# A two-layer transformer trunk in fp32 on one core: seven products of half blocks for eight in the last layer's second MLP product, and rotary tables loaded per layer

## The chip, the cores and the metric

The kernel runs on one core of one Trainium2 chip. The metric is the device time of one execution in microseconds. The kernel before takes 1665.89 us, the median of three runs (1664.36 to 1666.99).

## The reference

A latent stream x of 512 tokens and a context of 256 tokens, each 1024 wide, go through two layers. A layer normalises and modulates its input, projects it to three groups of attention heads (windowed, neighbourhood and latent), projects the heads' outputs back, and adds them with a gate. Then comes a squared-ReLU MLP of width 4096:

```python
def sq_relu_mlp(h, w1, w2):
    return jnp.square(jax.nn.relu(h @ w1)) @ w2
...
    x = x + mod_x[5] * sq_relu_mlp(modulate(rmsnorm(x, norm2_g[l]), mod_x[3], mod_x[4]),
                                   w_mlp_in[l], w_mlp_out[l])
    if not last:
        ctx = ctx + mod_c[5] * sq_relu_mlp(...)
return rmsnorm(x, final_norm_g)
```

In the last layer the context is not updated any more, so its MLP works on 512 tokens, in the first layer on 768. All data are float32.

## The kernel before

Each product of the large matrices is made of three matmuls, since TensorE gets operands in the shorter format fp32r: an operand is split into a high part (a cast on ACT) and a low part (the difference, on DVE), and high x high, high x low and low x high are added up in PSUM. `load_split` (L449) does that for a weight tile of 1024 columns: DMA to `raw`, ACT's cast to `wh` (L457), DVE's subtraction to `wl` (L458). The tiles `wh` and `wl` share a pool of five buffers, `w4`.

The MLP goes over 32 chunks of 128 hidden features in eight groups of four (L1054). `mlp1` makes a chunk: 24 matmuls in the last layer (8 pieces of the input, three each, L1083 to L1085) into a `psd` bank, then ReLU on ACT (L1090), the square on ACT as high part `uh` (L1091), the square on POOL (L1092) and the low part `ul` on DVE (L1093). `mlp2` makes a group's share of the second product: for each half of the 1024 output columns, four banks (`pss`, `pss`, `psv`, `psa`), one for each 128 tokens, get 4 chunks x 3 matmuls of 512 columns each (L1117 to L1119), that is 96 in a group. `resid` (L716) then multiplies a bank by the gate on DVE (L719) and adds it to x on POOL (L720). The loop at the end issues `mlp1(g + 1)` ahead of `mlp2(g)`. The last group goes through a path of its own (L1124), token tile by token tile, with split weights `wfh`, `wfl`.

A scheduler that is part of the build orders the instructions of each engine, from the order of the program, the buffers of the pools (`CAPS`) and its own estimate of durations; on the chip each engine works through its list in that order and waits at semaphores. So a change of a pool's size moves instructions in the whole program. `FENCE` delays a few DMAs at the start by a DVE copy of one column. The rotary table and the mask of the windowed heads are loaded once, in layer 0, to the pool of constants (`const`, L145, and L850).

```python
        mlp1(0)
        for g in range(NG):
            if g + 1 < NG:
                mlp1(g + 1)
            if g == 0:
                gates = load_gate(l, 5, 1 if last else 2)
            mlp2(g)
```

## Time and profile before

| | |
|---|---|
| median of three runs | 1665.89 us |
| profiled execution | 1664.7 us, of it a span of 1662.8 us |
| PE (matmul) busy | 1615.0 us, 97%, 8994 instructions |
| DVE busy | 1010.4 us, 61% |
| ACT busy | 684.2 us, 41% |
| POOL busy | 610.5 us, 37% |
| mean granted TensorE clock | 0.994 |
| chain that ended last | PE 89%, DVE 6%, DMA 2%, ACT 1% |

The span is the time from the first to the last instruction; the execution's time lies 1.9 us above it. Busy shares are averages over stages that have different limits. PE, DVE, ACT and POOL are TensorE's matmuls, VectorE, ScalarE and GpSimd. L12 is line 12 of the kernel. The chain of work that ended last is followed back from the last instruction, at each step to what released it.

### The profile page before, as it was taken

What the parts mean: (1) busy time and instruction counts of PE and PEld (TensorE: products, weight loads), DVE (VectorE), ACT (ScalarE), POOL (GpSimd) and SP (SyncE); (2) the same over time, 40 slices, a digit from 0 to 9 for tenths busy, and PEclk for the clock granted to TensorE, in tenths of its full rate; (3) what the DMA queues carried; (4) which work ended last, traced back from release to release, by engine and by line L of the source; (5) the groups of instructions that cost most, each with busy time, mean ns of one, the idle gap of its engine ahead of it and who ended that gap; (6) DMA issues with size and microseconds to landing.
All of it is one profiled execution on the core that took longest, in us unless ns stands there. A gap on an engine that the chain in (4) does not pass through costs nothing.

```text
span 1662.8 us, 24078 instructions
## 1 busy us (share of the span) xinstructions
PE 1615.0 (97%) x8994; PEld 1354.3 (81%) x8994; DVE 1010.4 (61%) x1995; ACT 684.2 (41%) x1342; POOL 610.5 (37%) x564
## 2 busy tenths in 40 slices
PE   6999999999899999999999999999999899999997
PEld 3888788776798988988989789878776788888886
DVE  3665865687787576444544866786686643344445
ACT  4544466656631312212223155536755522233332
POOL 1111643553433353341533441153453333333335
PEclk9999999999999999999999999999999999999999
DMA  9553411220154333334333712221120233333331
GB/s 319 179 167 112 134 35 26 67 65 13 33 184 134 120 115 114 115 102 125 90 106 116 236 51 74 62 60 39 42 82 15 66 98 91 102 101 97 93 106 72
DMA packets 156422, 164.47 MB, mean 99 GB/s; under 512 B 8960, under 2 KB 111368, under 8 KB 156304
## 3 DMA queue, kind: packets, MB, share of 16 engines
q1 hardware_dynamic: 156304, 162.92, 32.1%
q8 instruction: 71, 1.16, 0.3%
q14 instruction: 47, 0.39, 0.1%
HBM read 155.53 MB, written 2.12 MB: 95 GB/s over the span
## 4 chain that ended last, share of the span: by engine, by line
PE 89%; DVE 6%; DMA 2%; ACT 1%; issue 1%; POOL 0%; SPq 0%; POOLq 0%; DVEq 0%; ACTq 0%
PE psd L1083 9%; PE psd L1084 9%; PE psd L1085 9%; PE psv L669 5%; PE pss L611 5%; PE pst L660 5%; PE pss L1117 3%; PE pss L1118 3%; PE pss L1119 3%; PE psd L474 3%; PE psd L475 3%; PE psd L476 3%; PE pst L1119 2%; PE pst L1118 2%; PE psv L1118 2%; PE psv L1119 2%
## 5 line engine op out<-in xcount | busy, mean ns | idle before, releaser
L720 POOL TENSOR_TENSOR xlat<-xlat,rtmp 128x512 f32<-128x512 f32 x159 | 234.3, 1497 | 267.7 <-DVE rtmp L719 264.5
L458 DVE TENSOR_TENSOR wl<-raw,wh 128x1024 fp32r<-128x1024 f32 (+1 forms) x168 | 219.1, 1305 | 184.0 <-issue 72.2
L457 ACT CAST wh<-raw 128x1024 fp32r<-128x1024 f32 (+1 forms) x168 | 174.8, 1041 | 301.1 <-PE pst L1119 175.4
L1083 PE MATMUL psd<-hT,wh 128*128 128x384 f32 (+2 forms) x752 | 264.8, 353 | 3.9 <-DVE hT L421 3.9
L1084 PE MATMUL psd<-hT,wl 128*128 128x384 f32 (+2 forms) x752 | 264.2, 351 | 2.5 <-DVE wl L458 2.5
L1085 PE MATMUL psd<-hT,wh 128*128 128x384 f32 (+2 forms) x752 | 265.2, 353 | 0.1
L635 POOL TENSOR_TENSOR prob<-prob,sm 128x512 f32<-128x512 f32 (+3 forms) x110 | 126.9, 1161 | 256.3 <-DVE sm L628 175.8
L1092 POOL TENSOR_TENSOR relu<-relu 128x384 f32<-128x384 f32 (+1 forms) x96 | 97.6, 1018 | 314.1 <-ACT uh L1091 299.6
L1090 ACT ACTIVATE relu<-psd 128x384 f32<-128x384 f32 (+1 forms) x93 | 49.1, 528 | 279.4 <-PE psd L1085 276.4
L627 ACT ACTIVATE prob<-prob,m 128x513 f32<-128x513 f32 (+6 forms) x160 | 121.2, 758 | 94.3 <-DVE m L622 69.2
L1083 PEld LDWEIGHTS psd<-hT,wh 128*128 128x128 f32 x752 | 141.4, 188 | 15.7 <-DVE hT L421 4.4
L1093 DVE TENSOR_TENSOR ul<-relu,uh 128x384 fp32r<-128x384 f32 (+1 forms) x96 | 59.2, 617 | 152.7 <-POOL relu L1092 152.7
L1084 PEld LDWEIGHTS psd<-hT,wl 128*128 128x128 f32 x752 | 141.4, 188 | 12.8 <-DVE wl L458 3.2
L1085 PEld LDWEIGHTS psd<-hT,wh 128*128 128x128 f32 x752 | 141.3, 188 | 9.7 <-DVE hT L423 0.3
L282 DVE SCALAR_TENSOR_TENSOR acc<-araw,consts,acc 128x512 f32<-128x512 f32 x140 | 116.9, 860 | 15.0 <-DMA araw<-in_w_ada_dram 14.0
L660 PEld LDWEIGHTS pst<-consts,prob 128*128 128x128 f32 x688 | 77.8, 141 | 48.3 <-issue 37.5
L660 PE MATMUL pst<-consts,prob 128*128 128x128 f32 x688 | 114.2, 282 | 2.4 <-POOL prob L635 1.3
L476 PE MATMUL psd<-hT,wl 128*128 128x384 f32 (+1 forms) x280 | 97.1, 347 | 1.1 <-DVE wl L458 1.1
L474 PE MATMUL psd<-hT,wh 128*128 128x384 f32 (+1 forms) x280 | 97.8, 349 | 0.2 <-DVE rtmp L719 0.2
L475 PE MATMUL psd<-hT,wh 128*128 128x384 f32 (+1 forms) x280 | 97.1, 347 | 0.0
L664 ACT COPY pT<-pst 128x512 f32<-128x512 f32 x124 | 70.9, 585 | 62.8 <-PE pst L660 62.6
L1118 PE MATMUL pss<-wl,uh 128*128 128x512 f32 x224 | 87.4, 390 | 0.0
(265 smaller groups left out, 3576.9 us busy)
## 6 DMA issues: line engine op xcount, KB each, us to landing
raw<-in_w_mlp_in_dram SPq DMA_DIRECT2D x64, 512.0 KB, 4.0
raw<-in_w_mlp_out_dram SPq DMA_DIRECT2D x64, 512.0 KB, 3.8
araw<-in_w_ada_dram SPq DMA_DIRECT2D x112, 256.0 KB, 4.7
raw<-in_w_in_dram SPq DMA_DIRECT2D x24, 512.0 KB, 5.3
raw<-in_w_ada_dram SPq DMA_DIRECT2D x24, 512.0 KB, 3.9
raw<-in_w_ada_dram SPq DMA_DIRECT2D x32, 256.0 KB, 5.7
raw<-in_w_out_dram SPq DMA_DIRECT2D x8, 512.0 KB, 3.7
raw<-in_w_out_dram SPq DMA_DIRECT2D x16, 256.0 KB, 3.7
```

The costliest lines, as they stand in the source:

```text
L457: A.copy(hi, raw)
L458: V.tensor_tensor(lo, raw, bc(hi), ALU.subtract)
L474: T.matmul(ps[:, :n], wh[:, k, :], hh[k][:, s0:s0 + n], start=(k == 0), stop=False)
L475: T.matmul(ps[:, :n], wh[:, k, :], hl[k][:, s0:s0 + n], start=False, stop=False)
L476: T.matmul(ps[:, :n], wl[:, k, :], hh[k][:, s0:s0 + n], start=False, stop=(k == KC - 1))
L635: G.tensor_tensor(p_[:, :w_], p_[:, :w_], sm.to_broadcast([P, w_]), ALU.mult)
L660: T.transpose(pt[:, r * P:(r + 1) * P], pts[r][:, pos[r][kb]:pos[r][kb] + P], ident)
L720: (V if fast and (RLAST if fast == "end" and t == 3 else RFAST)[dh] == "V" else G).tensor_tensor(xt[t][:, cs], xt[t][:, cs], tmp, ALU.add)
L1083: T.matmul(o_, wh[:, k, :], hh[k][:, sl], start=(k == 0), stop=False)
L1084: T.matmul(o_, wl[:, k, :], hh[k][:, sl], start=False, stop=False)
L1085: T.matmul(o_, wh[:, k, :], hl[k][:, sl], start=False, stop=(k == KC - 1))
L1118: T.matmul(a_, uh[:, ts_], wl[:, c % 2, :], start=False, stop=False)
```

## The change

In seven of the eight groups of the last layer, two chunks of features and two token halves form a 2 x 2 block of the left matrix (token halves of 256, a11 and a12 the first half of the tokens, chunk by chunk), and two chunks and two column halves of the weights a 2 x 2 block of the right one (b11 and b12 the first chunk, column half by column half). Their product is made by the scheme of Strassen in Winograd's form: seven products of half blocks, four sums on the left and four on the right. `left_seven` and `right_seven` are generators that give one split operand at a time; the left sums and three of the right ones are made on POOL, one of the right ones on DVE. `product` adds the two pairs of chunks of a group in PSUM: 2 pairs x 2 banks x 3 matmuls = 12, seven times a group. Products go by turns to two banks `pss` and to the banks `psv` and `psa`; three of them are copied out by ACT to `pc` tiles (L1226), and the sums that Winograd's form needs at the end are made by further accumulation in the bank and by DVE (L1231). Gate and addition to x follow as before, by new lines (L1236 on DVE, L1237 on POOL) or by `resid`.

`uh` is now the full square of the chunk, made on POOL alone; there is no `ul` in these groups. The weights are loaded to `raw2` tiles. Splits of 256 columns go to `left` tiles (six), of 512 columns to `right` tiles (six). `w4` has four buffers for five, the split input of the MLP is two tiles in place of sixteen, attention outputs have a pool of their own, and rotary table and mask are loaded in each layer to `rA`, behind a copy of one column. The diff, cut:

```diff
-CAPS = {"tm": 4, "rt": 4, "pr": 8, "r0": 16, "re": 9, "raw": 4, "w4": 5, "pT": 4, "xn": 12,
-        "h1": 16, "h2": 16, "pg": 18, "cr": 1, "ct": 8, "kr": 5, "vc": 2, "kc": 8,
-        "up": 4, "u": 16, "wf": 16, "of": 8, "fg": 2, "ga": 4}
+CAPS = {"tm": 4, "rt": 4, "pr": 8, "r0": 16, "re": 9, "raw": 4, "w4": 4, "pT": 4, "xn": 12,
+        "h1": 16, "h2": 2, "pg": 18, "cr": 1, "ct": 8, "kr": 5, "vc": 2, "kc": 8,
+        "up": 4, "u": 16, "ls": 6, "rs": 6, "rw": 6, "pc": 7, "ts": 2, "wf": 16, "of": 8, "fg": 2, "ga": 4, "ot": 8, "rA": 1}
...
-FENCE = {"pw0": 4, "pw1": 6, "w3": 24, "w4": 30, "rA": 31, "mA": 31}
+FENCE = {"pw0": 4, "pw1": 6, "w3": 24, "w4": 4, "rA": 31, "mA": 31}
...
         xns = [norm_xn(g) for g in (groups if (l, which) != (0, 1) else groups[:1])]
         cols = mod_cols(l, which)
         ntok = P * sum(len(g) for g in groups)
-        hh = [page(ntok, F32R, f"hT{which}") for _ in range(KC)] if (l, which) != (0, 1) else []
-        hl = [page(ntok, F32R, f"hT{which}") for _ in range(KC)] if (l, which) != (0, 1) else []
+        hh, hl = [], []
+        if which == 2:
+            hh, hl = [[t_[:, k * ntok:(k + 1) * ntok] for k in range(KC)]
+                      for t_ in (page(KC * ntok, F32R, "hT2"), page(KC * ntok, F32R, "hT2"))]
+        elif l:
+            hh = [page(ntok, F32R, "hT1") for _ in range(KC)]
+            hl = [page(ntok, F32R, "hT1") for _ in range(KC)]
...
         def new_ot(c):
-            OT[c] = (page(nq, F32R, "oth"), page(nq, F32R, "otl"))
+            OT[c] = page2(nq, "ot")
...
         att_B(0)
-        if l == 0:
-            rA = const([2, 512], ropeA, "ropeA")
-            maskA = const([3, P], maskA_in, "maskA")
+        tabA = page(1408, name="ropeA")
+        rA, maskA = view(tabA[:, :1024], [2, 512]), view(tabA[:, 1024:], [3, P])
+        for t_, src, key in ((rA, ropeA, "rA"), (maskA, maskA_in, "mA")):
+            if l == 0:
+                fence(t_[:, 0], key)
+            else:
+                V.tensor_copy(t_[:, 0, 0:1], bc(KB[0][0][:, 0:1]))
+            nc.sync.dma_start(t_, src)
         proj_B(1)
         att_B(1)
         proj_AK()
...
         F0 = [sum(GSZ[:i]) for i in range(len(GSZ))]
         us = {}
 
+        def seven(g):
+            return last and g < len(GSZ) - 1
         def mlp1_chunks(g, c_list):
             work = []
             for i, c in enumerate(c_list):
                 f0 = (F0[g] + c) * P
                 w = load_split(
                     [(ALLP, w_mlp_in[l, :, f0:f0 + P].rearrange("(k p) f -> p k f", p=P))], [KC, P])
-                uh = page(ntok, F32R, "uh")
-                ul = page(ntok, F32R, "ul")
+                if seven(g):
+                    uh, ul = page(ntok, F32, "uh"), None
+                else:
+                    uh, ul = page(ntok, F32R, "uh"), page(ntok, F32R, "ul")
                 us[g, c] = (uh, ul)
                 pss = [(ps_d() if i == 0 else ps_s(), s0, n) for s0, n in halves]
                 work.append((w, pss, uh, ul))
...
                     sl = slice(s0, s0 + n)
                     r_ = prob(n, name="relu")
                     A.activation(r_, ps[:, :n], AF.Relu)
+                    if ul is None:
+                        G.tensor_tensor(uh[:, sl], r_, r_, ALU.mult)
+                        continue
                     A.activation(uh[:, sl], r_, AF.Square)
                     G.tensor_tensor(r_, r_, r_, ALU.mult)
                     V.tensor_tensor(ul[:, sl], r_, bc(uh[:, sl]), ALU.subtract)
...
             T.matmul(a_, uh[:, ts_], wl[:, c % 2, :], start=False, stop=False)
             T.matmul(a_, ul[:, ts_], wh[:, c % 2, :], start=False, stop=fin)
 
+        def left_seven(g, q):
+            n = ntok // 2
+            u0, u1 = us[g, 2 * q][0], us[g, 2 * q + 1][0]
+            a11, a21, a12, a22 = u0[:, :n], u0[:, n:], u1[:, :n], u1[:, n:]
+            def split(src):
+                o_ = page(2 * n, F32R, "left")
+                A.copy(o_[:, :n], src)
+                V.tensor_tensor(o_[:, n:], src, bc(o_[:, :n]), ALU.subtract)
+                return o_
+            e_ = page(n, name="tsum")
+            G.tensor_tensor(e_, a21, a22, ALU.add)
+            yield split(a11)
+            G.tensor_tensor(a21, a11, a21, ALU.subtract)
+            G.tensor_tensor(a11, e_, a11, ALU.subtract)
+            yield split(a12)
+            yield split(a11)
+            yield split(e_)
+            G.tensor_tensor(a12, a12, a11, ALU.subtract)
+            yield split(a21)
+            yield split(a12)
+            yield split(a22)
+        def right_seven(g, q):
+            f0 = (F0[g] + 2 * q) * P
+            r_ = []
+            for dh in range(2):
+                r_.append(view(sbuf(1024, F32, "raw2"), [2, 512]))
+                if g < 2:
+                    V.tensor_copy(r_[dh][:, 0, 0:1], bc(hh[0][:, 0:1]))
+                nc.sync.dma_start(r_[dh], w_mlp_out[l, f0:f0 + 2 * P, dh * 512:(dh + 1) * 512]
+                                  .rearrange("(j p) n -> p j n", p=P))
+            b11, b21, b12, b22 = r_[0][:, 0], r_[0][:, 1], r_[1][:, 0], r_[1][:, 1]
+            def split(src):
+                o_ = page(1024, F32R, "right")
+                A.copy(o_[:, :512], src)
+                V.tensor_tensor(o_[:, 512:], src, bc(o_[:, :512]), ALU.subtract)
+                return o_
+            e_ = page(512, name="tsum")
+            yield split(b11)
+            G.tensor_tensor(b11, b12, b11, ALU.subtract)
+            V.tensor_tensor(e_, b22, b11, ALU.subtract)
+            yield split(b21)
+            yield split(e_)
+            G.tensor_tensor(b21, b21, e_, ALU.subtract)
+            yield split(b11)
+            G.tensor_tensor(b12, b22, b12, ALU.subtract)
+            yield split(b12)
+            yield split(b22)
+            yield split(b21)
+        def mlp2_seven(g):
+            nt = ntok // 256
+            n = ntok // 2
+            nq_ = GSZ[g] // 2
+            ops = [(left_seven(g, q), right_seven(g, q)) for q in range(nq_)]
+            def product(banks, first):
+                for q, (le, ri) in enumerate(ops):
+                    a_, b_ = next(le), next(ri)
+                    for t, ps in enumerate(banks):
+                        ah, al = a_[:, t * P:(t + 1) * P], a_[:, n + t * P:n + (t + 1) * P]
+                        more = dict(skip_group_check=True)
+                        T.matmul(ps, ah, b_[:, :512], start=(first and q == 0), stop=False, **more)
+                        T.matmul(ps, ah, b_[:, 512:], start=False, stop=False, **more)
+                        T.matmul(ps, al, b_[:, :512], start=False, stop=(q == nq_ - 1), **more)
+            def out(banks):
+                res = []
+                for ps in banks:
+                    res.append(page(512, name="pc"))
+                    A.copy(res[-1], ps)
+                return res
+            def add(kept, banks, r, dh):
+                for t, (k_, ps) in enumerate(zip(kept, banks)):
+                    V.tensor_tensor(k_, k_, ps, ALU.add)
+                    resid_in(k_, r * nt + t, dh)
+            def resid_in(k_, t, dh):
+                cs = slice(dh * 512, (dh + 1) * 512)
+                V.tensor_tensor(k_, k_, gates[0 if t < 4 else 1, dh], ALU.mult)
+                G.tensor_tensor(xt[t][:, cs], xt[t][:, cs], k_, ALU.add)
+            fx = [ps_s, ps_s, ps_s][:nt]
+            fy = [ps_v, ps_a] if nt == 2 else [ps_t, ps_t, ps_v]
+            x_ = [f() for f in fx]
+            product(x_, True)
+            p1 = out(x_)
+            y_ = [f() for f in fy]
+            product(y_, True)
+            add(p1, y_, 0, 0)
+            product(x_, False)
+            u2 = out(x_)
+            step(STEPS)
+            y_ = [f() for f in fy]
+            product(y_, True)
+            p5 = out(y_)
+            product(x_, False)
+            add(p5, x_, 1, 1)
+            product(y_, False)
+            add(u2, y_, 0, 1)
+            product(x_, False)
+            for t, ps in enumerate(x_):
+                resid(ps, nt + t, 0, gates)
+            step(STEPS)
         def mlp2(g):
+            if seven(g):
+                return mlp2_seven(g)
```

The order of POOL's instructions in the middle of the last layer's MLP, one group before: squares of four chunks (L1092), and eight additions to x (L720).

```order
L1092 TENSOR_TENSOR relu_14765<-relu_14765 128x512
L1092 TENSOR_TENSOR relu_14803<-relu_14803 128x512
L720 TENSOR_TENSOR xlat_69<-xlat_69,rtmp_14872 128x512
L720 TENSOR_TENSOR xlat_69<-xlat_69,rtmp_14875 128x512
L720 TENSOR_TENSOR xlat_69<-xlat_69,rtmp_14878 128x512
L720 TENSOR_TENSOR xlat_69<-xlat_69,rtmp_14881 128x512
L720 TENSOR_TENSOR xlat_69<-xlat_69,rtmp_14948 128x512
L720 TENSOR_TENSOR xlat_69<-xlat_69,rtmp_14951 128x512
L720 TENSOR_TENSOR xlat_69<-xlat_69,rtmp_14954 128x512
L720 TENSOR_TENSOR xlat_69<-xlat_69,rtmp_14957 128x512
L1092 TENSOR_TENSOR relu_14993<-relu_14993 128x512
L1092 TENSOR_TENSOR relu_15031<-relu_15031 128x512
```

And with the change, twelve rows of a group (uh: left operands, raw2: right operands, pc: products that were kept; L1116 is a chunk's square):

```order
L1162 TENSOR_TENSOR tsum_14315<-uh_13848,uh_13883 128x256
L1164 TENSOR_TENSOR uh_13848<-uh_13848 128x256
L1237 TENSOR_TENSOR xlat_69<-xlat_69,pc_13956 128x512
L1237 TENSOR_TENSOR xlat_69<-xlat_69,pc_13958 128x512
L1237 TENSOR_TENSOR xlat_69<-xlat_69,pc_14056 128x512
L1165 TENSOR_TENSOR uh_13778<-tsum_14296,uh_13778 128x256
L1193 TENSOR_TENSOR raw2_14301<-raw2_14303,raw2_14301 128x512
L1165 TENSOR_TENSOR uh_13848<-tsum_14315,uh_13848 128x256
L1237 TENSOR_TENSOR xlat_69<-xlat_69,pc_14058 128x512
L1199 TENSOR_TENSOR raw2_14303<-raw2_14303 128x512
L1193 TENSOR_TENSOR raw2_14320<-raw2_14322,raw2_14320 128x512
L1169 TENSOR_TENSOR uh_13813<-uh_13813,uh_13778 128x256
```

Between the additions to x stand the sums of the next group's operands now; of these twelve rows eight are new work.

The order of DVE's instructions in the same stretch before: weight splits (L458), low parts of the chunks (L1093) and gate products (L719).

```order
L1093 TENSOR_TENSOR ul_14359<-relu_14385,uh_14358 128x512
L458 TENSOR_TENSOR wl_14469<-raw_14466,wh_14468 128x1024
L1093 TENSOR_TENSOR ul_14397<-relu_14423,uh_14396 128x512
L458 TENSOR_TENSOR wl_14511<-raw_14508,wh_14510 128x1024
L1093 TENSOR_TENSOR ul_14435<-relu_14461,uh_14434 128x512
L458 TENSOR_TENSOR wl_14541<-raw_14538,wh_14540 128x1024
L1093 TENSOR_TENSOR ul_14473<-relu_14499,uh_14472 128x512
L458 TENSOR_TENSOR wl_14587<-raw_14584,wh_14586 128x1024
L719 TENSOR_TENSOR rtmp_14568<-pss_14504,gates_91 128x512
L719 TENSOR_TENSOR rtmp_14571<-pss_14505,gates_91 128x512
L719 TENSOR_TENSOR rtmp_14574<-psv_14506,gates_91 128x512
L458 TENSOR_TENSOR wl_14617<-raw_14614,wh_14616 128x1024
```

And with the change (L1159 splits a left operand, L1189 a right one, L1231 adds a PSUM bank to a kept product, L1236 multiplies by the gate):

```order
L1231 TENSOR_TENSOR pc_14056<-pc_14056,pss_13912 128x512
L1189 TENSOR_TENSOR right_14139<-raw2_13940,right_14139 128x512
L1236 TENSOR_TENSOR pc_14056<-pc_14056,gates_91 128x512
L1159 TENSOR_TENSOR left_14298<-uh_13778,left_14298 128x256
L1231 TENSOR_TENSOR pc_14058<-pc_14058,pss_13913 128x512
L1189 TENSOR_TENSOR right_14306<-raw2_14301,right_14306 128x512
L1159 TENSOR_TENSOR left_14317<-uh_13848,left_14317 128x256
L1236 TENSOR_TENSOR pc_14058<-pc_14058,gates_91 128x512
L1189 TENSOR_TENSOR right_14325<-raw2_14320,right_14325 128x512
L1231 TENSOR_TENSOR pc_14024<-pc_14024,psv_14028 128x512
L1159 TENSOR_TENSOR left_14342<-uh_13813,left_14342 128x256
L1231 TENSOR_TENSOR pc_14026<-pc_14026,psa_14029 128x512
```

The splits of the next group's first operands stand between the additions that close this group. By count, the whole program has 84 matmuls fewer (8400 to 8316), 204 instructions more on DVE (1786 to 1990), 182 more on ACT and 98 more on POOL.

## Rows read from the trace of the kernel before

**Rows 1.** The page: span, busy time and share of each engine xinstructions, clock by slice.

```profile
span 1662.8 us, 24078 instructions
...
PE 1615.0 (97%) x8994; PEld 1354.3 (81%) x8994; DVE 1010.4 (61%) x1995; ACT 684.2 (41%) x1342; POOL 610.5 (37%) x564
...
PEclk9999999999999999999999999999999999999999
```

**Rows 2.** Chain that ended last, second layer's MLP: start us, us, what.

```profile
1361.54 0.45 PE pss L1117 x2
1405.06 0.45 PE pss L1117 x2
...
1622.66 0.45 PE pss L1117 x2
```

**Rows 3.** Windows, same stage: length, busy (count) of PE, PEld, DVE, ACT, POOL, PEclk, DMA.

```profile
1340.00:1400.00 60.00, 60.00 (x267) 49.67 (x266) 23.45 (x26) 18.18 (x24) 19.43 (x15) 1.00 0.32 97
...
1580.00:1640.00 60.00, 60.00 (x267) 49.67 (x266) 28.65 (x35) 16.73 (x26) 25.17 (x20) 1.00 0.27 88
```

**Rows 4.** Groups of ACT by line and shape: xcount, busy us, mean ns, idle before.

```profile
L457 ACT CAST wh<-raw 128x1024 fp32r<-128x1024 f32 x160 | 167.8, 1049 | 301.1 <-PE pst L1119 175.4 <-PE psa L1119 100.5 <-DMA raw<-in_w_in_dram 7.2
L664 ACT COPY pT<-pst 128x512 f32<-128x512 f32 x124 | 70.9, 585 | 62.8 <-PE pst L660 62.6
...
L1090 ACT ACTIVATE relu<-psd 128x512 f32<-128x512 f32 x31 | 18.6, 600 | 101.8 <-PE psd L1085 101.8
...
L1134 ACT CAST wfh<-raw 128x512 fp32r<-128x512 f32 x16 | 9.4, 621 | 16.8 <-DMA raw<-in_w_mlp_out_dram 16.8
```

**Rows 5.** Timeline of POOL, second layer's MLP: start us, us, line, operation, tiles.

```profile
1303.20 0.74 POOL L423 TENSOR_TENSOR hT<-tf,hT 128x256 fp32r<-128x256 f32 x1 [0.96 <-DVE hT L421]
...
1319.10 2.04 POOL L1092 TENSOR_TENSOR relu<-relu 128x512 f32<-128x512 f32 x2 [4.94 <-ACT uh L1091]
1324.28 1.04 POOL L1092 TENSOR_TENSOR relu<-relu 128x512 f32<-128x512 f32 x1 [3.14 <-ACT uh L1091]
...
1358.95 6.07 POOL L720 TENSOR_TENSOR xlat<-xlat,rtmp 128x512 f32<-128x512 f32 x4 [6.43 <-DVE rtmp L719]
...
1625.97 2.20 POOL L720 TENSOR_TENSOR xlat<-xlat,rtmp 128x512 f32<-128x512 f32 x1 [1.92 <-DVE rtmp L719]
1629.40 1.29 POOL L720 TENSOR_TENSOR xlat<-xlat,rtmp 128x512 f32<-128x512 f32 x1 [1.23 <-DVE rtmp L719]
```

**Rows 6.** Timeline of DVE, same stage, same columns.

```profile
1309.37 0.43 DVE L423 TENSOR_TENSOR hT<-tf,hT 128x256 fp32r<-128x256 f32 x1
...
1359.54 0.69 DVE L719 TENSOR_TENSOR rtmp<-psv,gates 128x512 f32<-128x512 f32 x1
...
1624.60 0.69 DVE L1135 TENSOR_TENSOR wfl<-raw,wfh 128x512 fp32r<-128x512 f32 x1 [2.57 <-ACT wfh L1134]
...
1625.81 1.22 DVE L458 TENSOR_TENSOR wl<-raw,wh 128x1024 fp32r<-128x1024 f32 x1
1626.94 1.78 DVE L1135 TENSOR_TENSOR wfl<-raw,wfh 128x512 fp32r<-128x512 f32 x1
```

**Rows 7.** Timeline of PE: the last matmul of the program.

```profile
1653.55 0.39 PE L1147 MATMUL psa<-wfh,ul 128*128 128x512 f32 x1
```

**Rows 8.** Waits of PE: releaser, us in total, times, longest; the first two.

```profile
PE psa L255 <- DMA raw<-in_w_ada_dram: 13.7, 6, 9.5
PE psd L1083 <- DVE hT L421: 3.9, 2, 3.5
```

**Rows 9.** Timeline of PE at a wait, and the window behind it (columns of rows 3).

```profile
359.51 0.44 PE L660 MATMUL pst<-consts,prob 128*128 128x128 f32 x2 [1.34 <-POOL prob L635]
...
361.00:364.40 3.40, 3.40 (x15) 3.11 (x15) 3.12 (x14) 2.12 (x5) 2.24 (x2) 0.50 0.01 2
```

More of the change, by code (lines that the diff above doesn't have):

```diff
@@ L58 @@
     ("h2", "hT2"),
-    ("pg", "qs kh kl vtok bias oth otl"),
+    ("pg", "qs kh kl vtok bias"),
     ("cr", "craw"),
@@ L68 @@
     ("ga", "gate"),
+    ("ot", "ot"),
+    ("rA", "ropeA"),
+    ("ls", "left"),
+    ("rs", "right"),
+    ("rw", "raw2"),
+    ("pc", "pc"),
+    ("ts", "tsum"),
 ):
@@ L97, in sbuf @@
         tag = TAGS[name]
-        size = 768 if tag in PAD else 512 if tag in PAD5 else -(-n // 256) * 256
+        size = 1536 if tag in ("ot",) else 768 if tag in PAD else 512 if tag in PAD5 else -(-n // 256) * 256
         return sb.tile([P, size], dt, tag=tag, name=name, bufs=CAPS[tag])[:, :n]
@@ L102, in page, with page2 @@
         return sbuf(n, dt, name)
+    def page2(n, name):
+        t_ = sbuf(2 * n, F32R, name)
+        return t_[:, :n], t_[:, n:2 * n]
     def temp(n, dt=F32, name="tmp"):
@@ L140, in ps_a @@
         return pp.tile([P, 512], F32, tag="a", name="psa", bufs=PS["a"])
-    call = cp.tile([P, 2304], F32, name="consts")
+    call = cp.tile([P, 896], F32, name="consts")
     c_off = [0]
@@ L151, in const @@
                 "p (a b c) -> p a b c", a=shape[0], b=shape[1])
-        if name in ("ropeA", "maskA"):
-            fence(t_[:, 0], "rA" if name == "ropeA" else "mA")
         nc.sync.dma_start(t_, src)
```

## The prediction

> **What bounds the kernel now.** I read the page first, then the chain that ended last, then the busy time of each engine in windows of the second layer's MLP, then the timelines of the two engines that get new work there. The page [rows 1] says that TensorE is busy for 97% of the span at a granted clock of nine tenths or more in every slice. The chain [rows 2] shows the stage that is changed as a clockwork: the first product of the second MLP matrix comes every 43.52 us, seven times. One such group has 96 matmuls of the first product and 96 of the second, so a matmul of 512 columns costs 43.52/192 = 0.2267 us. In the windows [rows 3] PE is busy for 60.00 of 60 us at clock 1.00, DVE for 23 to 29 us, ACT for 17 to 18, POOL for 19 to 25. So every matmul that goes shortens the stage, as long as the others keep up. The question is what the others are asked to do in its place.
>
> **Matmuls removed.** Seven of the eight groups go from 96 to 84 matmuls in the second product: 7 x 12 = 84 fewer, and the order of instructions has just that (8400 before, 8316 after). 84 x 0.2267 = 19.0 us. If nothing else mattered, a group would take 180 x 0.2267 = 40.8 us.
>
> **Work added, per group of the last layer.** For two pairs of chunks there are 14 left operands of 256 columns and 14 right ones of 512, each split by a cast on ACT and a subtraction on DVE. DVE also makes 2 right sums, 6 additions of PSUM to a kept product and 6 multiplications by the gate, and keeps 4 splits of 1024 columns and 2 gate products from PSUM; it loses 4 splits of 1024, 4 of 512 and 6 gate products. POOL keeps 4 squares and 8 additions to x, and gets 8 sums of 256 columns and 6 of 512.
>
> ACT is covered: 14 x 0.41 (an estimate, on the line through the 0.62 us cast of 512 and the 1.05 us cast of 1024 columns) + 14 x 0.62 + 6 x 0.59 + 4 x 1.05 + 4 x 0.60 = 24.5 us [rows 4], against 40.8 us of matmuls. If that cover went, ACT would cost nothing still, since DVE's list is longer.
>
> DVE and POOL look covered too when each is taken alone, but they are not alone. Look at four operations near the end [rows 5, 6]. POOL's addition to x, which takes 1.29 us by itself, starts at 1625.97 while DVE's split of 1024 columns runs from 1625.81 to 1627.03, and takes 2.20 us, to 1628.17. DVE's next split, 0.69 us by itself, starts at 1626.94 and takes 1.78 us, to 1628.72. They ran one after the other: 1.14 us of POOL after DVE's end, 0.55 us of DVE after POOL's. What hangs there is a DVE instruction that reads two SBUF tensors. The gate product, which reads PSUM and SBUF, takes its usual 0.69 us at 1359.54 in the middle of POOL's additions. So per group I add up POOL's 26 instructions and those 40 of DVE that read two SBUF tensors, as one queue.
>
> By themselves: DVE 14 x 0.43 + 22 x 0.69 + 4 x 1.22 = 26.1 us, POOL 8 x 0.74 + 14 x 1.29 + 4 x 1.04 = 28.1 us, together **54.2 us**. Where they alternate, each costs 0.14 to 0.15 us less, as above: 66 x 0.145 = 9.6 us off, **44.6 us**, if the queue never pauses. Both ends are above the 43.52 us that a group takes now, and above the 40.8 us of its matmuls. Before the change the same account was 8 x 1.22 + 4 x 0.69 + 4 x 1.04 + 8 x 1.29 = 27.0 us, well hidden.
>
> Here a rule speaks against the change as well. The Trainium skill, "SBUF — State Buffer", section "SBUF: two separate sides", says that DVE and GpSimd share a pair of SBUF ports as an exclusive lock, taken by a DVE instruction with two SBUF inputs against a GpSimd one that reads SBUF, and held for the whole instruction while the other blocks. By that wording a group costs the full 54.2 us; the rows show a handover 0.14 us before the recorded end.
>
> I take the middle, **49.4 us**: neither is the handover there for every instruction (40 of DVE cannot all alternate with 26 of POOL), nor is the queue free of pauses. DVE works in program order, and the order after the change puts an addition that waits for a PSUM bank, or a split that waits for ACT, in front of splits that PE waits for; POOL's sums of the next group stand behind DVE's first splits of it, since they overwrite the same data.
>
> **The sum.** The queue can start with the first square of the layer's MLP at 1319.1 [rows 5]. Seven groups: 7 x 49.4 = 345.8, to 1664.9. What the queue still has to do after the last split that PE waits for (about 10 us of gate products and additions) and what the eighth group asks of it before (4 squares and 12 splits of 512 columns, about 12 us) cancel within 2 us. Then PE has the seventh product and the whole last group: 96 x 0.2267 = 21.8 us, to 1686.7. It ended at 1653.9 before [rows 7], so +32.8 us. The tail behind the last matmul (8.9 us to the end of the span) is the same code. 1664.7 + 32.8 = 1697.5; the profiled execution is 1.2 us under the median, so I say **1698**. The ends: 44.6 us gives 1319.1 + 312.2 + 21.8 = 1653.1 and 1664; 54.2 us gives 1720.3 and 1731.
>
> **The other edits.** Rotary tables and mask now come twice, in their own buffer: 0.7 MB more of DMA and two DVE copies of one column, long before their use in the next projection; nothing. In layer 1 the copy waits for the keys of the first heads, which the attention in front of it has used. Split weights have four buffers for five in the whole kernel: the cast of the pair after next must wait for the pair in use, and has one pair's matmuls (24 to 48, 5.4 us and more) to hide a cast of 1.05 and a split of 1.22 us. Only where four buffers serve one stage at once can PE see it; 2.3 us at four such places would be 9 us above. Below, the scheduler's new order can win a few of PE's waits, the longest of which, after the first DMAs, is 3.9 us in all [rows 8]. I take 0 between -6 and +9. The attention outputs get a pool of their own, which only loosens waits. The fence of the weight load w4 moves nothing ahead of the first DMAs that PE waits for [rows 8]: in SP's list the four loads that follow them only change places.
>
> **Rivals.**
> 1. **The matmuls stay the bound** (faster). The chain has only PE in it, and the shares of DVE (61%) and POOL (37%) seem to leave room. It holds if the joint queue takes less than 40.8 us a group; then 1664.7 - 19.0 = 1646. Against it: the floor is 44.6 us, and no pair of such instructions in these rows overlaps. 0.12.
> 2. **Queue at its floor**: perfect alternation and no pause, 1664, that is no change. 0.08.
> 3. **The lock without early handover**, 54.2 us a group, 1731. Its page is named above. The measured 1.14 and 0.55 us speak against it, pauses of the queue bring the same time. 0.08.
> 4. **PE slows as well**: with 40.8 us of work in 49.4 PE now idles 8.6 us a group. After a wait of 1.34 us at 359.5 the granted clock was 0.50 (its level of 1.2 GHz) for 3.4 us [rows 9]. One or two such stretches a group, where PE is what is waited for, cost 1.7 us each: 7 x 1.7 to 7 x 3.4 = 12 to 24 us more, 1710 to 1722. It decides only if they fall in the first product, where DVE waits for weight buffers. 0.14.
>
> That the change does less than it says can be left out: the order shows the 84 matmuls gone.
>
> **How the numbers follow.** The forecast has 0.58. Faster by over 0.2% (about what a measurement can tell from no change, 3.3 us): rival 1 and a little, 0.13; within 0.2%: 0.07; slower: 0.80. The range reaches from the floor with a small gain elsewhere, 1660, to 1731, the upper end of the queue; rival 1 and a pile of rivals 3 and 4 stay out.
>
> **What would show it.** Right: the distance between the first products of two groups is 47 to 52 us in place of 43.52; DVE's splits of 512 columns take on average about 1 us for 0.69 and POOL's instructions are stretched likewise; PE idles in front of products for a split of DVE, 6 to 10 us a group; POOL's busy time in the stage is near 70%. Wrong: a distance of 41 us with PE without gaps (rival 1), or DVE and POOL instructions of this kind that overlap at their lone durations. A granted clock under 1.00 for several us in each group would be rival 4. If the stage is as forecast and the total is not, the difference lies before 1300 us, in the four weight buffers.

## The result, and the profile after

The changed kernel takes 1711.18 us (median of four runs, 1710.01 to 1712.64), the kernel before 1665.12 in the same session: 1.0277 times as long, 95% interval 1.0259 to 1.0294. The forecast was 1698, between 1660 and 1731. So sign and range hold, and the forecast is 13 us too low. The page of after, against [rows 1]:

```profile
span 1708.2 us, 24418 instructions
...
PE 1614.5 (95%) x8910; PEld 1343.8 (79%) x8910; DVE 1215.2 (71%) x2201; ACT 748.8 (44%) x1524; POOL 757.7 (44%) x662
...
PEclk8999999999999999999999999999999999999989
```

PE falls from 97% to 95%, DVE rises from 61% to 71%, POOL from 37% to 44%. The span is 45.4 us longer. To see where, I cut the last layer's MLP, from its first matmul to the end of the last one, at first products of the second matrix (windows; columns of rows 3). Before, the cuts lie at the first and the seventh group:

```profile
1296.37:1349.10 52.73, 48.48 (x267) 41.47 (x266) 29.13 (x45) 26.32 (x45) 14.90 (x17) 1.00 0.31 90
1349.10:1610.30 261.20, 261.20 (x1154) 216.26 (x1153) 106.17 (x120) 75.47 (x97) 97.78 (x72) 1.00 0.32 97
1610.30:1653.94 43.64, 43.64 (x193) 35.81 (x191) 28.40 (x38) 11.24 (x24) 20.52 (x17) 1.00 0.21 73
```

and after, since the order differs, at the second and the seventh group (so only the sums of the three windows can be compared):

```profile
1308.13:1396.65 88.52, 81.43 (x396) 68.95 (x397) 69.94 (x89) 43.97 (x84) 54.78 (x47) 0.96 0.40 119
1396.65:1631.31 234.66, 212.04 (x902) 171.03 (x901) 224.40 (x242) 111.77 (x220) 178.43 (x126) 0.97 0.30 90
1631.31:1698.24 66.93, 58.26 (x228) 44.85 (x226) 53.63 (x69) 19.22 (x43) 41.75 (x30) 0.92 0.06 22
```

Before, the MLP starts at 1296.37 and takes 357.57 us; after, it starts at 1308.13 and takes 390.11. So **11.8 us** are lost ahead of it, **32.5 us** in it, and 1.1 us behind the last matmul (9.96 us to the end of the span, 8.86 before): 45.4 in all. Inside it PE is idle for 390.11 - 351.74 = 38.4 us (4.3 before). Its 351.74 busy us are 17.47 more than the 353.31 of before less 84 x 0.2267 = 19.04: that is time at a lower granted clock, as the third column from the right shows (0.96, 0.97, 0.92 for 1.00). With the idle time, 34.11 + 17.47 - 19.04 = 32.54.

What PE waits for, in the stage (waits of PE, 1340 to 1680 us):

```profile
PE psd L1108 <- DVE wl L472: 18.0, 6, 6.0
PE pss L1218 <- DVE rtmp L733: 9.2, 4, 4.3
```

One such wait, where one group ends and the next begins. The window, then the timelines of DVE, POOL and PE:

```profile
1440.00:1450.00 10.00, 4.03 (x19) 3.02 (x17) 10.00 (x10) 1.84 (x3) 10.00 (x8) 0.80 0.00 0
```

```profile
1440.72 1.22 DVE L1236 TENSOR_TENSOR pc<-pc,gates 128x512 f32<-128x512 f32 x1
1441.87 1.23 DVE L1189 TENSOR_TENSOR right<-raw,right 128x512 fp32r<-128x512 f32 x1
1443.02 0.68 DVE L733 TENSOR_TENSOR rtmp<-pss,gates 128x512 f32<-128x512 f32 x1
1443.62 1.16 DVE L1236 TENSOR_TENSOR pc<-pc,gates 128x512 f32<-128x512 f32 x1
1444.70 1.48 DVE L1159 TENSOR_TENSOR left<-uh,left 128x256 fp32r<-128x256 f32 x1
...
1447.51 4.26 DVE L472 TENSOR_TENSOR wl<-raw,wh 128x1024 fp32r<-128x1024 f32 x2
```

```profile
1442.50 1.73 POOL L1237 TENSOR_TENSOR xlat<-xlat,pc 128x512 f32<-128x512 f32 x1
1444.19 1.71 POOL L734 TENSOR_TENSOR xlat<-xlat,rtmp 128x512 f32<-128x512 f32 x1
...
1447.27 1.44 POOL L1237 TENSOR_TENSOR xlat<-xlat,pc 128x512 f32<-128x512 f32 x1
```

```profile
1449.85 0.80 PE L1108 MATMUL psd<-hT,wl 128*128 128x512 f32 x1 [5.97 <-DVE wl L472]
```

DVE and POOL are both busy for all of the 10 us, and PE for 4.03. DVE's gate product (0.68 us by itself) takes 1.16 to 1.22, its split of 256 columns (0.41) 1.48, the two weight splits (1.22 each) 4.26 together. POOL's additions of 1.29 take 1.44 to 1.73, and two of them start 1.69 us apart with DVE's gate product between: 0.68 + 1.29 - 2 x 0.145 = 1.68. The gate products that read PSUM (L733) take 0.68, as they do alone. PE waits 5.97 us for the weight split, which stands behind all this in DVE's list, and the chain of waits lies on DVE from 1440.80 to 1449.80.

The same holds for the whole MLP. DVE's additions of a PSUM bank (L1231) and its gate products from SBUF (L1236) have the same shape and stand side by side in its list; durations in ns (least, median, greatest):

```profile
L1231 DVE TENSOR_TENSOR pc<-pc,pss x14: 674/678/687, 1382.5 to 1676.0; 128x512 f32<-128x512 f32 x14
L1236 DVE TENSOR_TENSOR pc<-pc,gates x42: 677/1176/1781, 1374.4 to 1680.2; 128x512 f32<-128x512 f32 x42
```

The other 28 additions from PSUM take 0.67 to 0.68, so all 42 take 0.67 to 0.69 us; the 42 products that read two SBUF tensors take up to 1.78.

A stretch at a lower clock can follow such a wait. In the chain that ended last (start us, us, what), behind the seventh group's first product, PE has waited 3.96 us for a weight split at 1648.51, and then a dozen matmuls follow each other every 0.43 us in place of 0.23; from 1648.5 to 1654.1 us the granted clock is 0.50 (1.2 GHz):

```profile
1646.25 2.21 DVE wl L472
1648.51 0.80 PE psd L1108
1649.30 0.43 PE psd L1109
```

### The profile page after: what moved, and what is told of

The parts are those of the page before. It is cut to its first block, busy times and chain, and to the rows that moved or that the text cites. A ratio compares the mean times of both kernels' runs of the same rounds, so it can differ in the third digit from the quotient of the medians.

```text
span 1708.2 us, 24418 instructions
## 1 busy us (share of the span) xinstructions
PE 1614.5 (95%) x8910; PEld 1343.8 (79%) x8910; DVE 1215.2 (71%) x2201; ACT 748.8 (44%) x1524; POOL 757.7 (44%) x662
## 4 chain that ended last, share of the span: by engine, by line
PE 78%; DVE 14%; DMA 3%; issue 3%; ACT 1%; POOL 0%; SPq 0%; POOLq 0%; DVEq 0%; ACTq 0%
PE psd L1108 8%; PE psd L1109 7%; PE psd L1107 7%; PE psv L683 5%; PE pst L674 5%; PE pss L625 5%; PE psd L488 3%; PE psd L490 3%; PE psd L489 3%; DVE wl L472 2%; DVE right L1189 2%; DVE left L1159 2%; DMA raw<-in_w_ada_dram 2%; PE psd L715 2%; PE psd L717 2%
## 5 line engine op out<-in xcount | busy, mean ns | idle before, releaser
L472 DVE TENSOR_TENSOR wl<-raw,wh 128x1024 fp32r<-128x1024 f32 (+1 forms) x140 | 199.4, 1427 | 132.3 <-ACT wh L471 125.0
L471 ACT CAST wh<-raw 128x1024 fp32r<-128x1024 f32 (+1 forms) x140 | 145.7, 1041 | 332.1 <-PE pst L1145 172.3
L1108 PE MATMUL psd<-hT,wl 128*128 128x384 f32 (+2 forms) x752 | 268.4, 357 | 21.1 <-DVE wl L472 21.1
L1107 PE MATMUL psd<-hT,wh 128*128 128x384 f32 (+2 forms) x752 | 267.9, 357 | 7.4 <-DVE hT L435 4.2
L1109 PE MATMUL psd<-hT,wh 128*128 128x384 f32 (+2 forms) x752 | 268.5, 357 | 0.8 <-POOL hT L437 0.7
L734 POOL TENSOR_TENSOR xlat<-xlat,rtmp 128x512 f32<-128x512 f32 x117 | 177.8, 1538 | 188.1 <-DVE rtmp L733 183.8
L1107 PEld LDWEIGHTS psd<-hT,wh 128*128 128x128 f32 x752 | 143.3, 191 | 21.0 <-DVE hT L435 4.6
L1119 POOL TENSOR_TENSOR relu<-relu 128x384 f32<-128x384 f32 (+1 forms) x68 | 64.1, 945 | 214.1 <-ACT uh L1118 181.3
L1109 PEld LDWEIGHTS psd<-hT,wh 128*128 128x128 f32 x752 | 143.8, 191 | 11.3 <-POOL hT L437 1.2
L291 DVE SCALAR_TENSOR_TENSOR acc<-araw,consts,acc 128x512 f32<-128x512 f32 x140 | 133.0, 974 | 6.2 <-DMA araw<-in_w_ada_dram 5.4
L1120 DVE TENSOR_TENSOR ul<-relu,uh 128x384 fp32r<-128x384 f32 (+1 forms) x68 | 41.9, 618 | 60.8 <-POOL relu L1119 60.8
L1237 POOL TENSOR_TENSOR xlat<-xlat,pc 128x512 f32<-128x512 f32 x42 | 66.7, 1590 | 35.7 <-DVE pc L1236 35.7
```

The lines of the kernel that those rows point to most:

```text
L291: V.scalar_tensor_tensor(a_, raw, ct[:, k, w:w + 1], a_, ALU.mult, ALU.add)
L471: A.copy(hi, raw)
L472: V.tensor_tensor(lo, raw, bc(hi), ALU.subtract)
L734: (V if fast and (RLAST if fast == "end" and t == 3 else RFAST)[dh] == "V" else G).tensor_tensor(xt[t][:, cs], xt[t][:, cs], tmp, ALU.add)
L1107: T.matmul(o_, wh[:, k, :], hh[k][:, sl], start=(k == 0), stop=False)
L1108: T.matmul(o_, wl[:, k, :], hh[k][:, sl], start=False, stop=False)
```

## The experiments

Theory: in the last MLP, DVE (where it reads two SBUF tensors) and POOL are one queue, and its length sets the time; ahead of it, the four weight buffers cost the 11.8 us. Rivals: DVE is the bound by its own work; the order of its list and the waits for banks and buffers are; the 11.8 us come from the tables or from the new operands. Twelve kernels ran. "Starts" and "takes" are the first matmul and the length of the last MLP as above; "group" is the mean of the five distances between the first products of the second to the seventh group. Each ratio is to the kernel before as it was timed beside that run (1664.0 to 1665.7 us).

| | median us | ratio to before [95%] | starts | takes | group |
|---|---|---|---|---|---|
| before | 1665.12 | | 1296.4 | 357.6 | 43.5 |
| after | 1711.18 | 1.0277 [1.0259, 1.0294] | 1308.1 | 390.1 | 46.9 |
| 1 eight products | 1679.18 | 1.0083 [1.0055, 1.0111] | 1311.7 | 357.7 | 43.5 |
| 2 four buffers alone | 1683.05 | 1.0112 [1.0086, 1.0138] | 1315.2 | 359.4 | 43.5 |
| 3 additions to x on DVE | 1687.20 | 1.0136 [1.0113, 1.0160] | 1308.3 | 366.0 | 43.7 |
| 4 squares on ACT | 1706.84 | 1.0256 [1.0232, 1.0279] | 1307.6 | 386.6 | 47.0 |
| 5 no additions to x | 1671.42 | 1.0042 [1.0027, 1.0057] | 1308.1 | 351.3 | 42.0 |
| 6 later fence | 1710.46 | 1.0269 [1.0249, 1.0290] | 1311.1 | 389.1 | 47.3 |
| 7 sums in SBUF | 1695.17 | 1.0185 [1.0167, 1.0204] | 1321.2 | 361.3 | 42.9 |
| 8 run 3, five buffers | 1693.79 | 1.0178 [1.0157, 1.0199] | 1297.3 | 384.0 | 46.6 |
| 9 sums, fused | 1667.31 | 1.0017 [1.0008, 1.0026] | 1294.1 | 359.0 | 42.8 |
| 10 runs 3 and 4 | 1671.66 | 1.0041 [1.0026, 1.0056] | 1308.2 | 351.4 | 41.4 |
| 11 run 9, squares on POOL | 1666.74 | 1.0019 [1.0009, 1.0029] | 1294.4 | 357.1 | 41.6 |
| 12 run 11, right operands late | 1658.25 | 0.9958 [0.9945, 0.9972] | 1292.3 | 350.3 | 42.1 |

**1. The other edits without the seven products.**

```diff
         def seven(g):
-            return last and g < len(GSZ) - 1
+            return False
...
-        tabA = page(1408, name="ropeA")
+        if l == 0:
+            rA = const([2, 512], ropeA, "ropeA")
```

> The changed kernel with the eight products of before in every group, and with tables and mask loaded once as before; four weight buffers, the earlier fence, the MLP input in two tiles and the pool of the attention outputs stay. Theory: the 11 us that the changed kernel loses ahead of the last MLP come from these pools, so 1674 to 1679 us, and a group of the last MLP takes 43.5 us again. Rival: they come from the tables or from the operands of the seven products (buffers, order), so 1663 to 1668 us.

**2. The kernel before with four weight buffers.**

```diff
-"w4": 5
+"w4": 4
```

> The kernel before with four buffers for split weights in place of five, nothing else. Theory: this alone is most of the 11 us, 1671 to 1677 us. Rival: a pair of weights is always split in time, 1663 to 1668 us.

Both losses show with no seven products and no second load of tables in the program: 14.4 and 18.3 us, nearly all of it ahead of the last MLP, which takes 357.7 and 359.4 us (357.6 before). Run 1 ends at the upper end of what was expected, run 2 lies 6 us above it: the buffers alone cost no less than with the other edits beside them. PE's idle time up to there (windows, before and run 2):

```profile
60.00:1296.00 1236.00, 1216.38 (x6977) 1028.21 (x6978) 818.64 (x1720) 536.62 (x1109) 463.58 (x443) 0.99 0.30 92
```

```profile
60.00:1315.00 1255.00, 1224.58 (x6982) 1031.22 (x6980) 834.68 (x1723) 540.11 (x1110) 465.26 (x444) 0.99 0.30 91
```

19.6 us idle before, 30.4 in run 2; the other 8.2 us are longer busy time of the same matmuls. PE's waits for split weights are only a small part of it, 4.7 us in that window (3.2 before): behind the first DMAs the longest of its waits in run 2 are for others.

```profile
PE psd L288 <- DVE acc L282: 4.5, 2, 3.5
PE pst L660 <- POOL prob L635: 3.7, 2, 2.1
PE pss L611 <- DVE qs L551: 3.2, 3, 1.5
...
PE psd L702 <- DVE wl L458: 0.8, 1, 0.8
```

So it isn't the one stage that the prediction looked for. That four buffers change the order of the whole program, and that splits stand ahead of other work on DVE, would both look like this; no run told them apart.

**3. The additions to x on DVE.**

```diff
-                G.tensor_tensor(xt[t][:, cs], xt[t][:, cs], k_, ALU.add)
+                V.tensor_tensor(xt[t][:, cs], xt[t][:, cs], k_, ALU.add)
```

and the same for the two of `resid` in each of these groups.

> The changed kernel with the eight additions to x of each of the seven groups on DVE in place of POOL. Theory (DVE and POOL are one queue where both read SBUF): the queue loses 8 x (1.29 - 0.69) = 4.8 us a group though DVE gets 5.5 us more to do, 1711 - 34 = 1677 us, between 1670 and 1690. Rival 1 (DVE alone is the bound): 8 x 0.69 = 5.5 us a group more, about 1750 us. Rival 2 (order of DVE's list, waits for banks and buffers): within 5 us of 1711.

24 us faster (34 were expected), with more work on the engine that PE waits for. The same stretch after and in run 3:

```profile
1400.00:1600.00 200.00, 179.33 (x761) 144.64 (x760) 189.74 (x200) 87.89 (x172) 156.54 (x110) 0.97 0.31 92
```

```profile
1400.00:1600.00 200.00, 190.99 (x830) 154.45 (x829) 191.71 (x253) 100.07 (x193) 126.58 (x80) 1.00 0.33 97
```

POOL's busy time falls by 30 us, DVE's rises by 2 us only, although it makes 37 additions there, of 0.68 us by themselves: its other instructions are stretched less. PE gets 11.7 us more. DVE alone as the bound (1750 us) is out. Nor is it that somebody lacked what these additions give (x, or the `pc` tile that each frees). Of the changed kernel's 42 additions L1237 the profile says:

```profile
who waited for it (us, times):
  ACT right L1188: 2.6, 1
```

**4. The squares on ACT.**

```diff
-                        G.tensor_tensor(uh[:, sl], r_, r_, ALU.mult)
+                        A.activation(uh[:, sl], r_, AF.Square)
```

> The changed kernel with the squares of the chunks in the seven groups on ACT in place of POOL. Theory (one queue): 4 x 1.04 = 4.2 us of POOL less a group, 1711 - 29 = 1682 us, between 1680 and 1692. Rivals (DVE alone, or order and waits): POOL has idle time anyway, within 5 us of 1711.

A miss: 4.3 us faster, not 29. DVE gets 10.5 us free in that stretch (179.23 us busy of 200), and spends as much on waits for PE, which must free a weight buffer first:

```profile
DVE wl L472 <- PE psd L1108: 5.9, 1, 5.9
DVE wl L472 <- PE psd L1109: 4.5, 1, 4.5
```

From this I took it that the squares lie where DVE has room; run 10 tests that.

**5. No additions to x.**

```diff
-                G.tensor_tensor(xt[t][:, cs], xt[t][:, cs], k_, ALU.add)
```

> The changed kernel without the eight additions to x in the seven groups (left out: what these groups add to x). Theory (one queue of DVE and POOL): 8 x 1.29 = 10.3 us a group less, so that the 40.8 us of matmuls bound the group again or nearly (41 to 43 us): 1711 - 7 x 6.5 = 1665 us, between 1657 and 1675. Rival (DVE alone, or its order and the weight buffers): POOL's additions end no wait of PE, so above 1700 us.

39.8 us faster than the changed kernel, a group 42.0 us: the matmuls bound it nearly. The rival (above 1700) is out, though only one instruction waited for the 42 additions shown above.

**6. Right operands fenced later.**

```diff
-                    V.tensor_copy(r_[dh][:, 0, 0:1], bc(hh[0][:, 0:1]))
+                    V.tensor_copy(r_[dh][:, 0, 0:1], bc(hh[KC - 1][:, 0:1]))
```

> The changed kernel with the loads of the first two groups' right operands behind the last piece of the MLP's input (hT) in place of the first. Theory: the first splits of right operands, which stood in DVE's list ahead of the last pieces of hT, cost the start of the last MLP 5 to 7 us, so 1704 to 1706 us. Rival: the start is bound elsewhere, or what is put off is late for the first group, 1710 to 1714 us.

No difference. The fence names the last piece, but its first column: the first half of the tokens. The pieces of the second half come later; run 12 fences behind those.

**7. Sums in SBUF.** With `"w4": 5`, `hT2` in 16 tiles, `"u": 12`, `"re": 8`, `"ls": 5`, `"rs": 5`, `"rw": 4`, `"pc": 4`, the fence of run 6, squares on ACT, and for `out` and `add` (cut):

```diff
+            def acc(banks, r, dh):
+                for t, ps in enumerate(banks):
+                    key = (r * nt + t, dh)
+                    if key in xacc:
+                        V.tensor_tensor(xacc[key], xacc[key], ps, ALU.add)
+                    else:
...
+                        A.copy(xacc[key], ps)
...
+            if g == len(GSZ) - 2:
+                for (t, dh), a_ in xacc.items():
+                    cs = slice(dh * 512, (dh + 1) * 512)
+                    V.tensor_tensor(a_, a_, gates[0, dh], ALU.mult)
+                    G.tensor_tensor(xt[t][:, cs], xt[t][:, cs], a_, ALU.add)
```

> A version of the change with little work in the queue: six of the eight output tiles are summed up over the seven groups in SBUF, by DVE additions that read PSUM, and get gate and addition to x once behind the seventh group; the squares of the chunks are made on ACT. Five buffers for split weights, MLP input in 16 tiles, right operands fenced as in the run above, fewer buffers elsewhere to make room. Theory: the queue has 22.0 us on DVE and 16.3 on POOL a group, so the 40.8 us of matmuls bound it, and nothing is lost ahead of the last MLP: 1665 - 19 + 5 to 12 for the start, 1651 to 1660 us. Rival (order of DVE's list and buffers bound the group): 45 us and more a group, 1680 us and above.

A miss: 35 us above the upper end. The groups did what was expected up to the sixth (40.8 to 41.7 us; 49.1 from there to the seventh), the rest didn't. The last MLP starts 25 us later than before: I had made room with buffers that the first layer uses too, and PE waited there.

```profile
PE psd L297 <- DVE acc L291: 15.8, 3, 13.4
...
PE psd L317 <- DVE arow L314: 5.3, 2, 4.5
```

Run 9 gives most of these buffers back and starts at 1294.1.

**8. Run 3 with five weight buffers.** `"w4": 5`, `hT2` in 16 tiles, the fence of run 6, `"rw": 4`, `"rs": 5`, `"ls": 5`, `"pc": 5`, `"u": 14`, `"re": 8`, `"pg": 17`.

> The run with the additions to x on DVE, and with five buffers for split weights, MLP input in 16 tiles, the later fence, and fewer buffers for the operands (loads 4, right 5, left 5, kept products 5). Theory: 1687 less the 11 us of the four weight buffers and less 5 us of the start, about 1671 us, between 1665 and 1680. Rival (the seven products need their six buffers each): 1685 us and above.

The last MLP starts at 1297.3, as before the change: the 11 us are back with the fifth buffer. But it takes 384.0 us for 366.0, so the time is the rival's. What the 18 us come from is open: seven pools shrank at once, and the fence and the order changed. Four `left`, `right` and `raw2` tiles each are no hindrance by themselves: with sums in SBUF, runs 11 and 12 have 40.8 us a group with them.

**9. Sums fused with the last group.** Run 7 with `"u": 16`, `"re": 9`, `"of": 4`, without the pass behind the seventh group, and in the last group:

```diff
+                        if (t, dh) in xacc:
+                            V.tensor_tensor(xacc[t, dh], xacc[t, dh], a_, ALU.add)
+                            a_ = xacc[t, dh]
                         resid(a_, t, dh, gates, fast="end" if last else True)
```

> The run with sums in SBUF again, without what it lost outside the groups: 9 buffers for ReLU outputs and 16 for the chunks as in the changed kernel, and the six sums take up the last group's banks (one DVE addition from PSUM each) before gate and addition to x, in place of a pass of their own behind the seventh group. Theory: the first layer is as fast as before the change, the last MLP takes 329 us of matmuls, 9.4 us at its start as before, 5 us in the groups and 5 to 12 at its end, 349 to 356 us against 357.6: 1657 to 1664 us. Rival (its end or the fewer operand buffers cost what the matmuls save): 1666 us and above.

Ahead of the last MLP nothing is lost now (1294.1), but that takes 359.0 us, 3 us more than the upper end: the time is the rival's. Its groups are not to blame, from the second to the sixth PE is busy for 164.10 of 164.65 us; what is lost lies at the start and the end.

**10. Runs 3 and 4 together.** The diffs of both.

> The run with the additions to x on DVE (1687.2 us), with the squares of the chunks on ACT as well. Theory, as amended after the run with the squares alone: the squares fall into the first product, where DVE has room since it waits for weight buffers, so 1683 to 1689 us. Rival (one queue that never rests): down to the bound by matmuls, 1673 to 1678 us.

15.5 us faster than run 3: the amended theory, that the squares cost next to nothing, falls as well, and the queue that never rests is the nearer of the two, though the time is 1.3 us below its range. Beside POOL's additions the squares did not show; without these they do. Why they did not in run 4 is not shown: DVE waited there for weight buffers, and no run gave it more of them.

**11. Run 9 with the squares on POOL.** `"ls": 4`, `"rs": 4`, `"of": 8` besides.

> The first run of these three with the squares on POOL as in the changed kernel (right and left operands have four buffers each for five). Theory: the squares lie where DVE and POOL have room, within 3 us of that run. Rival (every instruction of the queue counts): the queue is 4.2 us longer a group, 39 us of 40.8 with its pauses, and 10 us or more are lost.

Here they cost nothing that shows, and the rival (10 us or more) is out. Its groups, from the first to the sixth, are 40.80 us apart each (44.8 from there to the seventh). A part of what is lost still lies at the start of the MLP, in DVE's list:

```profile
1310.11 0.69 DVE L1190 TENSOR_TENSOR right<-raw,right 128x512 fp32r<-128x512 f32 x1 [2.21 <-ACT right L1189]
1310.72 1.64 DVE L435 CAST hT<-tf 128x256 fp32r<-128x256 f32 x2
...
1314.98 3.49 DVE L1190 TENSOR_TENSOR right<-raw,right 128x512 fp32r<-128x512 f32 x3
1318.40 1.34 DVE L435 CAST hT<-tf 128x256 fp32r<-128x256 f32 x1
```

```profile
1311.06 0.39 PE L1108 MATMUL psd<-hT,wh 128*128 128x256 f32 x1 [1.22 <-DVE hT L435]
...
1319.80 0.39 PE L1108 MATMUL psd<-hT,wh 128*128 128x256 f32 x1 [2.66 <-DVE hT L435]
```

A split of a right operand waits 2.21 us for its cast, three more take 3.49 us, and the last pieces of hT stand behind them; PE waits 1.22 and 2.66 us for those.

**12. Right operands behind the first chunk's square.**

```diff
-                    V.tensor_copy(r_[dh][:, 0, 0:1], bc(hh[KC - 1][:, 0:1]))
+                    V.tensor_copy(r_[dh][:, 0, 0:1], us[0, 0][0][:, 0:1])
```

> The run with fused sums and squares on POOL (1666.7 us), with the loads of the first right operands behind a column of the first chunk's square in place of the MLP's input. Theory: in that run four splits of right operands, which waited for their DMA and the cast, stood in DVE's list between the last pieces of hT, and the first group's product came 7.9 us later than before the change; without them 5 to 8 us are won back: 1659 to 1662 us, below the 1664.4 of the kernel before. Rival (the start is bound by the norm's own chain, or the operands then come late for the first product): 1665 to 1668 us.

1658.25 against 1665.65 us for the kernel before: 0.9958 times, 0.9945 to 0.9972, and below the 1659 to 1662 that were expected. The three windows of its last MLP, cut at the first products of the second and the sixth group:

```profile
1292.25:1385.20 92.95, 89.32 (x447) 75.28 (x446) 69.48 (x97) 47.39 (x88) 54.57 (x47) 1.00 0.40 116
1385.20:1548.40 163.20, 163.20 (x721) 135.13 (x720) 149.87 (x192) 73.77 (x144) 103.07 (x80) 1.00 0.33 103
1548.40:1642.53 94.13, 86.21 (x361) 69.17 (x359) 76.38 (x113) 35.68 (x77) 46.10 (x35) 0.96 0.17 59
```

PE is busy for 163.20 of 163.20 us in four groups: 4 x 40.80. Behind them it still idles 7.9 us, 5.6 of it for ACT's casts of right operands.

## Why the prediction was right, and what it missed

- **Matmuls removed: right.** 40.8 us a group is what runs 11 and 12 show when nothing else is in the way. Of the 19.0 us in all, run 12 keeps 7.4.
- **ACT covered: right.** 87.9 busy us in the 200 from 1400 to 1600, that is 20.6 a group where the sum had 24.5.
- **DVE and POOL as one queue: right in mechanism.** Less work in the queue makes the kernel faster even where DVE gets more (run 3) and where hardly anything waits for what is left out (run 5), and what reads PSUM is not stretched. By the prediction's account a group would take 49.4 us after, 44.6 in runs 3 and 8, 45.5 in run 4, 39.7 in run 5, 40.7 in run 10 and 38.4 in run 11. Measured are 46.9, 43.7 and 46.6, 47.0, 42.0, 41.4, and 40.8 for most groups of run 11; where the account is below 40.8 the matmuls take over. It is right within 2.5 us, and it says when they do. It isn't good for differences: the squares alone should have given 3.9 us a group and gave nothing. That a queue which pauses for PE's weight buffers doesn't turn every microsecond into time would explain it, and is not shown. Nor is it good for one group: the five distances of after are 41.4 to 52.0 us, in part because the order puts 157 to 205 matmuls between two cuts and not 180 each time.
- **The sum for the stage: +32.8, measured +32.5; that they agree so well is luck.** A group is 46.9 us and not 49.4. Of the 34.1 + 17.5 = 51.6 us that PE's idle time and the lower clock cost in the stage, 5 x 6.13 = 30.6 lie in the five distances, and 21.0 outside them, where the sum had put nothing of its own: ahead of the second group's first product PE idles 7.1 us of 88.5 at a clock of 0.96, and behind the seventh group's 8.7 of 66.9 at 0.92, 7.6 of them for weight splits. At the start the order of DVE's list can cost several us, as run 12 shows for its own kernel (8.5 us); for the changed kernel that is not shown.
- **The other edits: the step that failed.** The prediction took 0 between -6 and +9 for them, and had four buffers in place of five down as hidden but for "2.3 us at four such places". It is 11.8 us here, 18.3 in run 2 with that edit alone, and no single wait: of the 11.8 us, 4.2 lie ahead of the first layer's MLP (its first matmul at 437.4 us, 433.2 before) and the rest in it. Tables for each layer, the pool of the attention outputs and the fence were rightly put at nothing: runs 8, 11 and 12 keep them, and their last MLP starts at 1292 to 1297 us. The input in two tiles was taken back in them together with the four buffers, and wasn't run alone. The 11.8 us and the 1.1 us behind the last matmul are the 13 us between 1698 and 1711.
- **The signs.** POOL's share of the stage (70%), the stretched splits of 512 columns (1.02 and 1.32 us on average from 1400 to 1600 us, by source) and PE's waits for DVE's splits are there. The distance is at the edge (46.9 for 47 to 52), and PE idles 4.5 us a group and not 6 to 10: the lower clock makes 1.6 us a group of the difference.
- **Rival 1** (matmuls the bound, 1646): out, by the groups' distance. **Rival 2** (the floor, 1664) and **rival 3** (the full durations, 1731): the measured group lies between 44.6 and 54.2, nearer to the floor. In the timelines above a product on DVE and an addition on POOL, 0.68 + 1.29 = 1.97 us one behind the other, take 1.69, so the handover ahead of the recorded end holds here too. The Trainium skill, "SBUF — State Buffer", section "SBUF: two separate sides", has the other engine blocked for the whole instruction, which would be the 1.97 us. **Rival 4** (lower clock on top, 1710 to 1722): the time that it gave is the nearest, and the clock did cost 17.5 us of busy time. Some of that lies on the path. The chain shown with the waits of PE goes through a dozen matmuls at half speed. How much of the 17.5 us ended on the path in all, no run told apart; that the 1711 lie in rival 4's range is due to the 11.8 us ahead of the stage.
- **Arithmetic.** Added up as written, 1697.5 and 1.2 are 1698.7 and not 1698, and the two ends leave the 1.2 out; nothing hangs on it.

## What to carry to other kernels

Where DVE instructions that read two SBUF tensors run beside POOL's, add both up as one queue before you trade matmuls for vector work, and compare that with what the matmuls of the stage take. Get work out of that queue by reading PSUM (an accumulator in SBUF that takes up banks), by summing up before scaling, or by giving POOL's work to DVE, which needs about half the time for it. A buffer taken from a pool that serves the whole program was paid for here far ahead of the stage that was changed: run such an edit alone before it is put down at nothing.

## What the runs showed of the hardware

More work for the busiest vector engine can make a kernel faster: in run 3 DVE got 8 x 0.69 = 5.5 us a group more, POOL lost 10.3, and the kernel won 24 us. What two edits of the same queue win doesn't add up: moving the squares won 4.3 us by itself and 15.5 us once the additions were gone from POOL. And a DVE instruction of the same shape is stretched or not by where its operands lie: 0.67 to 0.69 us in all 42 cases with a PSUM bank, 0.68 to 1.78 us with two SBUF tensors.
